# A two-layer hybrid decoder trunk on one core: the order of the memory pools, with TensorE's operands at multiples of 256 bytes

## The chip, the core and the metric

The kernel runs on one core of one Trainium2 chip. The metric is device time in microseconds for one execution, from launch to end; the median of three runs of the kernel before is 1096.18 us (1096.07 to 1096.39). Lower is better.

## The reference: what is computed

The input is one sequence of 512 tokens with 1024 channels in float32. Two layers follow each other. In each layer, `h = RMSNorm(x)`, one combined projection `p = h @ W_in` is cut into the inputs of three mixers and of three merge gates, and the layer ends with a residual:

```
yA = (silu(gate) * B * conv3(C * xA)) @ Wout_A                  # gated convolution of width 3
yB = (sparse attention, 8 heads of 64, times silu(gate)) @ Wout_B
yC = (pooling over windows 2/4/8/16, linear, scale, silu gate) @ Wout_C
x  = x + (sigmoid(gA)*yA + sigmoid(gB)*yB + sigmoid(gC)*yC) @ W_o
```

The attention has rotary positions and normalized queries and keys. A small indexer (8 heads) scores all earlier keys of a query, the 128 best are kept, and the softmax runs over those.

## The kernel before, in words

Everything is held transposed: channels on the 128 partitions, the 512 tokens along the free axis. A float32 product is made of three TensorE matmuls on float32r parts: each operand is split into a high part (a rounded copy) and a low part (the rest), and `mm3` adds high x high, high x low and low x high into one PSUM tile of 128 x 512. `mm` (line 385) issues each of them. In the profile's names, `pj<-xhi,whi` is a matmul into the PSUM tile `pj` whose moving operand is `xhi` (512 columns) and whose stationary operand, loaded by a separate LDWEIGHTS, is 128 columns (512 bytes of a partition) of `whi`.

The weights come as 90 chunks of 128 x 1024 float32 a layer, in their order of use. `prep` loads a chunk into `raw` on the SP queue, ScalarE copies it to `whi` (line 368) and VectorE makes `wlo` (line 369); two raw and three split chunks are held at a time. `project` multiplies one chunk with the eight k tiles of the layer's input: `xhi0..7` and `xlo0..7`, written by `load_x`, each 2048 bytes of a partition. That is 24 matmuls of 512 columns for a chunk, 65 times a layer. The output products of the three branches (`merge`) and of the layer (`project(src)`) take the same weights against tiles `b` (8192 bytes, four slices of 512 columns). The value projection ("v" below) turns this round: there `whi` and `wlo` move, 512 columns at a time, and 128-column slices of `xhi` and `xlo` are loaded as weights. The selection of keys (16 rounds of MAX8 and MATCH_REPLACE8 for each of three query blocks) and the splits run on VectorE beside the matmuls.

The order of instructions on each engine is not the program's: class `Order` plays a list schedule with costs for each instruction and fixes it with edges. It looks at tiles, tags and buffer numbers, and not at where a tile lies in memory.

A tile pool takes a stretch of each partition in the order in which the pools are opened, and in a pool each tag takes its buffers in the order of first use, each rounded up to 32 bytes. The first free byte is 16512. This gives these starts (bytes in a partition, and what is left over a multiple of 256):

| tile | start before | over 256 |
|---|---|---|
| ct (cos, sin, identity, ones, masks), 6212 bytes | 16512 | 128 |
| vt | 22752 | 224 |
| xhi0, xlo0, ss, xhi1, xlo1 ... (17 tiles, 2048 bytes apart) | 22976 | 192 |
| ob (the ones and block matrices) | 57792 | 192 |
| raw, whi, wlo (4096 bytes each) | 63584, 71776, 84064 | 96 |
| b (8 of 8192 bytes), k | 96352, 161888 | 96 |
| a, w, h | 178272, 186464, 200800 | 96 |
| z (3 of 2112 bytes) | 208992 | 96, 160, 224 |
| pth (2 of 6656 bytes) | 215328, 221984 | 32 |

The identity matrix of the transposes (line 388, `pt<-ct,a`) is a part of `ct` and begins at 20608, 128 over a multiple of 256.

Of the kernel before, what the change touches and what calls it, by code (L numbers as in the profile page):

```python
# [5 lines left out]
F32 = mybir.dt.float32  # L6
F32R = mybir.dt.float32r
AF = mybir.ActivationFunctionType
ALU = mybir.AluOpType
PSUM = bass.MemoryType.PSUM  # L10
# [3 lines left out]
P = 128  # L14
S = 512
# [6 lines left out]

# constant columns
C_COS, C_SIN, C_ID, C_ONE, C_BLK, C_CAU, C_INV, C_EPS, C_END = (
    0, 512, 1024, 1152, 1280, 1408, 1536, 1552, 1553)
# per-layer vector columns
V_G, V_CW, V_PS, V_QG, V_KG, V_END = 0, 8, 20, 24, 26, 28


class Order:  # L30
    """The order of the instructions on each engine: a list schedule of the traced program.

    An instruction's place is found from the data it needs, the slots its tiles need and what it
    costs; edges without semaphores then keep each engine to that order."""

    # us from the end of an instruction to the start of one that waits for it
    LAT = {"PE": 0.2, "DVE": 0.13, "Activation": 0.14, "Pool": 0.1, "SP": 0.13}
# [20 lines left out]
    @staticmethod  # L58
    def region(ap):
        """partitions and elements of a tile that an access touches"""  # L60
        t, ap, off = ap.tensor, [list(x) for x in ap.ap], ap.offset
        row = 1
        for n in t.shape[1:]:
            row *= n
        if ap[0][0] != row:
            return t.name, (0, 1 << 30), {0: None}
        p, f = divmod(off, row)
        mask = 1
        for step, n in ap[1:]:
            m = 0  # L70
            for i in range(n):
                m |= mask << (i * step)
            mask = m
        return t.name, (p, p + ap[0][1]), mask << f
# [33 lines left out]
    def cost(self, inst, kind):  # L108
        """us on the engine, and us until the result is there"""
        def size(a):  # L110
            n = 1
            for _, k in a.bass_ap.ap[1:]:
                n *= k
            return n

        aps = [a for a in inst.ins if hasattr(a, "bass_ap")]
        out = inst.outs[0]
        n = size(out)
        psum = any(a.bass_ap.tensor.name.split("_")[0] in ("pj", "sc", "pt", "pv") for a in aps)
        wide = [a for a in aps if size(a) > 1]  # L120
        extra = len(aps) > len(wide)
        engine = str(inst.engine).split(".")[-1]
        if kind == "InstMatmult":
            f32 = str(aps[0].dtype).endswith("float32")
            c = (0.0004167 * n + 0.003) * ((4 if n > 128 else 2) if f32 else 1)
            return c, 0.0
        if kind == "InstDMACopy":
            b = n * out.bass_ap.ap[0][1] * 4
            return (0.65 if aps[0].bass_ap.tensor.name in self.slot else 0.48), b / 360e3
        if engine == "Activation":  # L130
            return 0.093 - 0.042 * psum + 0.000833 * n + 0.093 * extra, 0.0
        if engine == "Pool":
            return (0.1 if kind == "InstMemset" else 0.1 + 0.0022 * n), 0.0
        if kind in ("InstMax", "InstMatchReplace"):
            return 0.069 + 0.00104 * max(size(a) for a in aps), 0.0
        fast = kind == "InstTensorScalarPtr" and len(wide) == 1 and not psum
        return 0.069 + 0.00104 * n * (0.5 if fast else 1) + 0.061 * extra, 0.0
# [109 lines left out]
    def arrange(self, passes=PASSES):  # L247
        raw = self.read()
        ops, users, seqs, place = [], {}, {}, {}
# [23 lines left out]
        for k in range(passes):  # L273
            total, begin, end, order, why = self.play(ops, costs, succ, prio, users)
            if best is None or total < best[0]:
                best = (total, order, begin, end)
            # when each instruction has to start so that the tensor engine never waits
            need = [0.0] * n
# [24 lines left out]
def trunk(ctx, tc, xT, wst, vecs, cst, outT):  # L303
    nc = tc.nc
    order = Order(tc)
    pool = lambda name, bufs, **kw: order.pool(ctx.enter_context(tc.tile_pool(name=name, bufs=bufs, **kw)), name, bufs)
    cp = pool("cp", 1)
    wp = pool("wp", 3)
    bp = pool("bp", 8)
    wk = pool("wk", 7)  # L310
    sm = pool("sm", 4)
    pp = pool("pp", 4, space=PSUM)
    dp = pool("dp", 1, space=bass.MemoryType.DRAM)

    dve, act, pe, gp = nc.vector, nc.scalar, nc.tensor, nc.gpsimd

    ct = cp.tile([P, C_END], F32, name="ct")
    vt = cp.tile([P, DEPTH, V_END], F32, name="vt")
# [7 lines left out]
    def nm(s):  # L326
        uid[0] += 1
        return f"{s}_{uid[0]}"
# [24 lines left out]

    # ---- weight stream: chunks in their order of use, split into two float32r parts
    wq = {}
# [24 lines left out]
    def evac(out, ps, by):  # L380
        """PSUM to SBUF"""
        dve.tensor_tensor(out=out, in0=ps, in1=by, op=ALU.mult)  # L382
# [20 lines left out]
    def mm2(ps, lhs, src):  # L403
        """product with a matrix of ones and zeros"""
        hi, lo = W(F32R), W(F32R)
        split(hi, lo, src)
        mm(ps, lhs, hi, True, False)
        mm(ps, lhs, lo, False, True)
# [3 lines left out]
    def load_x(l, k, xt):  # L412
        """the two parts of x*g for the projections, and the running sum of squares"""
        g = vt[:, l, V_G + k:V_G + k + 1]
        hi = cp.tile([P, S], F32R, name=nm("xhi"), tag=f"xhi{k}")
        lo = cp.tile([P, S], F32R, name=nm("xlo"), tag=f"xlo{k}")
        split(hi, lo, xt, g)
        xh[k] = (hi, lo)
        sq = A()
        act.activation(sq, xt, AF.Square)  # L420
        if k == 0:
            xh["ss"] = cp.tile([P, S], F32, name=nm("ss"), tag="ss")
            gp.tensor_copy(xh["ss"], sq)
        else:
            gp.tensor_tensor(out=xh["ss"], in0=xh["ss"], in1=sq, op=ALU.add)

    def rsqrt(dst, ps, inv_n):
        """the table's value and a Newton step"""
        s, y, h = W(), W(), W()
# [7 lines left out]

# [1 line left out]
    load(vt, vecs)  # L439
# [21 lines left out]
    def wavefront(n, src, head):  # L461
        """n projections at once, whose last source tile comes late"""
        ws = [take() for _ in range(n)]
# [8 lines left out]
    for l in range(DEPTH):  # L472
        # ---- index projections
        ps_ik, pa0, pb0 = wavefront(3, lambda k: xh[k], l == 0)
# [3 lines left out]
        def rope(A, B, c, s, gA=None, gB=None):  # L478
            """-> A*c - B*s, B*c + A*s"""
            t = [W() for _ in range(4)]  # L480
# [17 lines left out]
        def move(pairs):  # L498
            """copies between partitions"""
            for d, u in pairs:  # L500
                load(d.bitcast(F32), u.bitcast(F32))
# [6 lines left out]

        # the indexer's r of the query is left to iw: relu(r s) w = relu(s) (r w)
        iq = [stack(*rope(pa0, pb0, cos, sin))]  # L510
# [8 lines left out]
        pa = project()  # L519
        # ik: x1 in rows 0:32, x2 in rows 32:64; iw in rows 64:72  # L520
        tk = [W() for _ in range(4)]
# [15 lines left out]
        def columns():  # L537
            """r and the heads' weights with tokens on partitions"""
            pw = pt()
# [9 lines left out]

        # ---- index scores and the selection, as an additive bias per query block  # L550
        bias = [cau] + [cp.tile([P, (b + 1) * P], F32, name=nm("score"), tag=f"score{b}") for b in range(1, 4)]
# [25 lines left out]
        def silu2(ps, out=None):  # L577
            """2 * silu(r * ps)"""
            g = W()
# [30 lines left out]

        # ---- pooling branch
        pwh, pwl = take()
# [39 lines left out]

        # ---- queries, keys, values
        def normed(gcol, then):
# [35 lines left out]

        # v, tokens on partitions; a head's 128 columns are [hi lo]
        vps = [pj(), pj(), pj(), pv()]
# [16 lines left out]
        def attention(qd, q, khh, kll):  # L709
            pts, prs = {}, {}  # L710

            def scores(j, b):
# [6 lines left out]
                mn = sm.tile([P, 1], F32, name=nm("mn"), tag="mn")  # L719
                # -(s + bias)/8, and its minimum  # L720
                dve.tensor_tensor_reduce(out=pr[:, :w], in0=ps[:, :w], in1=bias[b], scale=-0.125, scalar=3.0e38,  # L721
# [7 lines left out]
            def turn(j, b):  # L729
# [4 lines left out]
                for c in range(b + 1):  # L734
                    transpose(pst[:, c, :], pr[:, c * P:(c + 1) * P])
                # block (b, c) lies at 3c + b
                dh, dl = (t[:, b:b + 3 * b + 1:3, :] for t in pts[j])
# [28 lines left out]

        # ---- gate of the attention branch (its output replaces it)
        yb = big(F32)
# [5 lines left out]

        # ---- convolution branch
        yh, yl = big(), big()
# [32 lines left out]

        # ---- output projection and residual  # L810
        src = lambda k: (mh[k // 4][:, k % 4, :], ml[k // 4][:, k % 4, :])
# [19 lines left out]
def _columns():  # L831
    """column numbers of w_in, a list of 128 (or fewer) per projection tile, in their order of use"""
    import numpy as np
# [107 lines left out]
```

## Time and profile before

| | |
|---|---|
| median of the runs, us | 1096.18 |
| span of the profiled execution, us | 1093.9 |
| TensorE (PE) busy, us | 1082.8 |
| TensorE weight load (PEld) busy, us | 877.7 |
| VectorE (DVE) busy, us | 800.0 |
| ScalarE (ACT) busy, us | 465.8 |
| GpSimd (POOL) busy, us | 96.9 |
| DMA, mean GB/s | 114 |

The profiled execution's own time is its span, 1093.9 us, and about 2.3 us around it that the records don't cover (the runs agree within 0.3 us of each other). The busy time of PE counts each matmul from its start to its modelled end; matmuls overlap, so a single one shows 390 to 400 ns while the next one starts after 225 to 240 ns. The distance from one start to the next, called the pitch below, is what a matmul costs in a dense stretch.

### The profile page before, as it was taken

What the parts mean: (1) busy time and instruction counts of PE and PEld (TensorE: products, weight loads), DVE (VectorE), ACT (ScalarE), POOL (GpSimd) and SP (SyncE); (2) the same over time, 40 slices, a digit from 0 to 9 for tenths busy, and PEclk for the clock granted to TensorE, in tenths of its full rate; (3) what the DMA queues carried; (4) which work ended last, traced back from release to release, by engine and by line L of the source; (5) the groups of instructions that cost most, each with busy time, mean ns of one, the idle gap of its engine ahead of it and who ended that gap; (6) DMA issues with size and microseconds to landing.
All of it is one profiled execution on the core that took longest, in us unless ns stands there. A gap on an engine that the chain in (4) does not pass through costs nothing.

```text
span 1093.9 us, 13444 instructions
## 1 busy us (share of the span) xinstructions
PE 1082.8 (99%) x4842; PEld 877.7 (80%) x4842; DVE 800.0 (73%) x1389; ACT 465.8 (43%) x747; POOL 96.9 (9%) x76
## 2 busy tenths in 40 slices
PE   7999999999999999999999999999999999999998
PEld 5788888888888888888887778888888878888887
DVE  6989999987558865455559899999776498744442
ACT  6355222485223673233334542235852347623320
POOL 4000000000000011221310000000000001121310
PEclk9999999999999999999999999999999999999999
DMA  6542222452224522234535322225423245132252
GB/s 222 162 128 78 96 97 95 132 147 70 82 98 130 160 72 80 94 97 161 166 116 150 116 84 94 96 78 163 126 77 97 78 138 151 59 96 96 96 192 77
DMA packets 44402, 124.39 MB, mean 114 GB/s; under 512 B 6960, under 2 KB 7472, under 8 KB 44336
## 3 DMA queue, kind: packets, MB, share of 16 engines
q1 hardware_dynamic: 44336, 123.53, 35.9%
q8 instruction: 38, 0.62, 0.2%
q14 instruction: 28, 0.23, 0.1%
HBM read 101.49 MB, written 4.19 MB: 97 GB/s over the span
## 4 chain that ended last, share of the span: by engine, by line
PE 97%; DVE 1%; DMA 1%; ACT 1%; SPq 0%; issue 0%; DVEq 0%
PE pj L385 88%; PE sc L385 4%; PE pv L385 3%; PE pt L388 2%; DMA b<-in_x 0%; DVE wlo L369 0%; SPq L352 0%; DMA k<-h 0%; ACT xhi L400 0%; ACT whi L368 0%; DVE h L398 0%; DVE xlo L401 0%; ACT a L420 0%; DVE w L646 0%; DVE w L816 0%
## 5 line engine op out<-in xcount | busy, mean ns | idle before, releaser
L385 PE MATMUL pj<-xhi,whi 128*128 128x512 f32 x1040 | 378.1, 398 | 6.2 <-ACT whi L368 6.2
L385 PE MATMUL pj<-xhi,wlo 128*128 128x512 f32 x1040 | 377.5, 397 | 0.2 <-DVE wlo L369 0.2
L385 PE MATMUL pj<-xlo,whi 128*128 128x512 f32 x1040 | 377.3, 397 | 0.0
L368 ACT ACTIVATE whi<-raw 128x1024 fp32r<-128x1024 f32 (+2 forms) x185 | 191.6, 1037 | 403.0 <-PE pj L385 362.9
L369 DVE TENSOR_TENSOR wlo<-raw,whi 128x1024 fp32r<-128x1024 f32 (+2 forms) x185 | 227.7, 1233 | 18.2 <-ACT whi L368 17.2
L385 PEld LDWEIGHTS pj<-xhi,whi 128*128 128x128 f32 x1040 | 194.8, 188 | 50.6 <-ACT whi L368 6.2
L385 PEld LDWEIGHTS pj<-xlo,whi 128*128 128x128 f32 x1040 | 195.2, 188 | 45.5 <-DVE xlo L401 0.5
L385 PEld LDWEIGHTS pj<-xhi,wlo 128*128 128x128 f32 x1040 | 195.3, 188 | 45.3 <-DVE wlo L369 1.4
L385 PE MATMUL pj<-b,whi 128*128 128x512 f32 x640 | 211.2, 391 | 0.0
L382 DVE TENSOR_TENSOR w<-pj,ss 128x512 f32<-128x512 f32 x104 | 71.0, 686 | 99.8 <-PE pj L385 99.0
L385 PEld LDWEIGHTS pj<-b,whi 128*128 128x128 f32 x640 | 119.9, 188 | 25.4
L385 PE MATMUL pj<-b,wlo 128*128 128x512 f32 x320 | 118.5, 392 | 0.0
L607 POOL TENSOR_TENSOR b<-b,w 128x512 f32<-128x512 f32 x32 | 60.7, 1904 | 269.4 <-DVE w L605 269.2
L385 PEld LDWEIGHTS pj<-b,wlo 128*128 128x128 f32 x320 | 60.0, 188 | 12.7
L573 DVE MAX8 m<-score 128x8 f32<-128x256 f32 (+2 forms) x96 | 53.2, 558 | 1.7
L574 DVE MATCH_REPLACE8 score<-m,score 128x384 f32<-128x384 f32 (+2 forms) x96 | 52.1, 543 | 0.0
L739 DVE TENSOR_TENSOR pth<-pt,pth 128x128 fp32r<-128x128 f32 (+1 forms) x64 | 31.1, 486 | 19.0 <-PE pv L385 9.5
L816 DVE TENSOR_TENSOR w<-pj,w 128x512 f32<-128x512 f32 x16 | 11.0, 690 | 45.6 <-PE pj L385 45.6
L724 ACT ACTIVATE a<-a,mn 128x128 f32<-128x128 f32 (+1 forms) x64 | 35.7, 558 | 16.0 <-DVE mn L721 15.5
L662 POOL TENSOR_TENSOR w<-w,w 128x512 f32<-128x512 f32 x8 | 11.3, 1414 | 333.1 <-ACT w L661 333.1
L738 ACT ACTIVATE pth<-pt 128x128 fp32r<-128x128 f32 (+1 forms) x64 | 27.7, 433 | 28.2 <-PE pt L388 20.6
L385 PE MATMUL pv<-pth,b 128*128 128x512 f32 (+3 forms) x128 | 39.7, 314 | 0.0
(119 smaller groups left out, 1002.0 us busy)
## 6 DMA issues: line engine op xcount, KB each, us to landing
raw<-in_w SPq DMA_DIRECT2D x177, 512.0 KB, 3.3
b<-h SPq DMA_DIRECT2D x128, 64.0 KB, 2.3
k<-h SPq DMA_DIRECT2D x64, 128.0 KB, 3.0
b<-in_x SPq DMA_DIRECT2D x8, 256.0 KB, 4.8
w<-in_x SPq DMA_DIRECT2D x8, 256.0 KB, 5.6
xs<-w SPq DMA_DIRECT2D x8, 256.0 KB, 2.4
w<-xs SPq DMA_DIRECT2D x8, 256.0 KB, 4.1
out_x<-w SPq DMA_DIRECT2D x8, 256.0 KB, 2.0
```

The source lines that it names most:

```text
L368: act.activation(hi[:, p], raw[:, p], AF.Copy)
L369: dve.tensor_tensor(out=lo[:, p], in0=raw[:, p], in1=hi[:, p].bitcast(F32), op=ALU.subtract)
L382: dve.tensor_tensor(out=out, in0=ps, in1=by, op=ALU.mult)
L385: pe.matmul(ps, lhs, rhs, start=start, stop=stop)
L388: pe.transpose(out, src, ident if n == P else ident[64:64 + n, 64:64 + n])
L573: dve.max(m8, score)
L574: dve.match_replace(score, m8, score, -3.0e38)
L607: gp.tensor_tensor(out=a, in0=a, in1=g, op=ALU.add)
L662: gp.tensor_tensor(out=s0, in0=s0, in1=s1, op=ALU.add)
L724: act.activation(pr[:, :w], pr[:, :w], AF.Exp, bias=mn, scale=-1.0, accum_out=zs)
L738: act.activation(dh, pst[:, :b + 1, :], AF.Copy)
L739: dve.tensor_tensor(out=dl, in0=pst[:, :b + 1, :], in1=dh.bitcast(F32), op=ALU.subtract)
```

## The change

The pools are opened in another order. A new pool `xp` comes first; it holds one tile `gap` of 128 bytes that nothing writes or reads, and then the tiles `xhi`, `xlo` and `ss`, which were in `cp`. `wp`, `bp` and `wk` follow, and `cp` with the constants stands behind them. The rest of the diff takes comments out of the source.

```diff
@@ trunk
-    cp = pool("cp", 1)
+    xp = pool("xp", 1)
     wp = pool("wp", 3)
     bp = pool("bp", 8)
     wk = pool("wk", 7)
+    cp = pool("cp", 1)
     sm = pool("sm", 4)
...
+    xp.tile([P, 32], F32, name="gap")
     ct = cp.tile([P, C_END], F32, name="ct")
...
@@ load_x
-        hi = cp.tile([P, S], F32R, name=nm("xhi"), tag=f"xhi{k}")
-        lo = cp.tile([P, S], F32R, name=nm("xlo"), tag=f"xlo{k}")
+        hi = xp.tile([P, S], F32R, name=nm("xhi"), tag=f"xhi{k}")
+        lo = xp.tile([P, S], F32R, name=nm("xlo"), tag=f"xlo{k}")
...
-            xh["ss"] = cp.tile([P, S], F32, name=nm("ss"), tag="ss")
+            xh["ss"] = xp.tile([P, S], F32, name=nm("ss"), tag="ss")
```

By the same counting of sizes, the tiles then start here:

| tile | start after | over 256 |
|---|---|---|
| xhi0, xlo0, ss, xhi1 ... (2048 bytes apart) | 16640 | 0 |
| raw, whi, wlo | 51456, 59648, 71936 | 0 |
| b, k | 84224, 149760 | 0 |
| a, w, h | 166144, 174336, 188672 | 0 |
| z | 196864 | 0, 64, 128 |
| pth | 203200, 209856 | 192 |
| ct, vt, ob | 216512, 222752, 222976 | 192, 32, 0 |

No instruction is added, removed or reshaped, and `Order` sees the same tiles, tags and buffer numbers.

## Rows read from the trace of the kernel before

**Rows 1.** The page, parts 1 and 2: PE, and TensorE's granted clock in tenths.
```profile
PE 1082.8 (99%) x4842; PEld 877.7 (80%) x4842; DVE 800.0 (73%) x1389; ACT 465.8 (43%) x747; POOL 96.9 (9%) x76
PEclk9999999999999999999999999999999999999999
```

**Rows 2.** The page, part 4: the chain that ended last, by engine and line.
```profile
PE 97%; DVE 1%; DMA 1%; ACT 1%; SPq 0%; issue 0%; DVEq 0%
PE pj L385 88%; PE sc L385 4%; PE pv L385 3%; PE pt L388 2%; DMA b<-in_x 0%; DVE wlo L369 0%; SPq L352 0%; DMA k<-h 0%; ACT xhi L400 0%; ACT whi L368 0%; DVE h L398 0%; DVE xlo L401 0%; ACT a L420 0%; DVE w L646 0%; DVE w L816 0%
```

**Rows 3.** Waits of PE: waited for, us in total, times, longest.
```profile
PE pj L385 <- ACT whi L368: 6.2, 1, 6.2
```

**Rows 4.** Groups by form, PE and PEld: output<-moving,stationary, shapes, count | busy us, mean ns.
```profile
L385 PE MATMUL pj<-xhi,whi 128*128 128x512 f32 x1040 | 378.1, 398 | 6.2 <-ACT whi L368 6.2
L385 PE MATMUL pj<-b,whi 128*128 128x512 f32 x640 | 211.2, 391 | 0.0
L385 PE MATMUL pj<-b,wlo 128*128 128x512 f32 x320 | 118.5, 392 | 0.0
L385 PE MATMUL pj<-whi,xhi 128*128 128x512 f32 x48 | 17.7, 395 | 0.0
L385 PE MATMUL pv<-whi,xhi 128*128 128x512 f32 x16 | 6.3, 396 | 0.0
L388 PE MATMUL pt<-ct,a 128*128 128x128 f32 x160 | 28.0, 272 | 0.2
L385 PEld LDWEIGHTS pj<-xhi,whi 128*128 128x128 f32 x1040 | 194.8, 188 | 50.6 <-ACT whi L368 6.2
```

**Rows 5.** Timeline of PE, projections alone (start us, us); 15 starts from first to last.
```profile
324.64 0.40 PE L385 MATMUL pj<-xhi,whi 128*128 128x512 f32 x1
...
328.14 0.40 PE L385 MATMUL pj<-xhi,whi 128*128 128x512 f32 x1
```

**Rows 6.** Timeline of PE, output projection alone; 12 starts from first to last.
```profile
544.17 0.39 PE L385 MATMUL pj<-b,wlo 128*128 128x512 f32 x1
...
546.89 0.39 PE L385 MATMUL pj<-b,wlo 128*128 128x512 f32 x1
```

**Rows 7.** Timeline of PE, value projection alone; 14 starts from first to last.
```profile
187.65 0.40 PE L385 MATMUL pv<-whi,xlo 128*128 128x512 f32 x1
...
190.93 0.40 PE L385 MATMUL pv<-whi,xhi 128*128 128x512 f32 x1
```

**Rows 8.** Timeline of PE, both kinds by turns, one matmul each; 14 starts.
```profile
182.57 0.39 PE L385 MATMUL pj<-whi,xhi 128*128 128x512 f32 x1
182.79 0.40 PE L385 MATMUL pj<-xlo,whi 128*128 128x512 f32 x1
...
185.79 0.39 PE L385 MATMUL pj<-wlo,xhi 128*128 128x512 f32 x1
```

**Rows 9.** Timeline of PE: four transposes in a row.
```profile
410.94 0.60 PE L388 MATMUL pt<-ct,a 128*128 128x128 f32 x4
```

**Rows 10.** Windows of 25 us: window, length, busy of PE, PEld, DVE, ACT, POOL.
```profile
0.00:25.00 25.00, 18.56 (x70) 13.91 (x71) 17.59 (x18) 16.61 (x29) 11.63 (x14) 1.00 0.68 231
75.00:100.00 25.00, 25.00 (x116) 20.50 (x116) 24.01 (x43) 16.06 (x31) 0.30 (x3) 1.00 0.19 64
125.00:150.00 25.00, 25.00 (x109) 20.24 (x109) 23.86 (x56) 6.36 (x8) 0.00 (x0) 1.00 0.27 87
150.00:175.00 25.00, 25.00 (x109) 20.19 (x109) 24.11 (x50) 6.36 (x7) 0.00 (x0) 1.00 0.30 103
175.00:200.00 25.00, 25.00 (x109) 20.18 (x108) 24.24 (x41) 10.49 (x15) 2.60 (x2) 1.00 0.28 85
200.00:225.00 25.00, 25.00 (x111) 20.26 (x111) 24.22 (x45) 12.86 (x20) 0.00 (x0) 1.00 0.63 174
675.00:700.00 25.00, 25.00 (x110) 20.21 (x109) 24.19 (x52) 7.84 (x9) 0.00 (x0) 1.00 0.26 91
725.00:750.00 25.00, 25.00 (x108) 20.10 (x108) 24.81 (x41) 10.97 (x15) 1.54 (x1) 1.00 0.41 123
875.00:900.00 25.00, 25.00 (x107) 19.82 (x106) 24.21 (x34) 8.66 (x12) 1.55 (x1) 1.00 0.43 126
```

## The prediction, made blind

> **What bounds the kernel now.** First the page's shares: TensorE has work in 99% of the span, and its granted clock is full, the level of 2.4 GHz, in all 40 slices [rows 1]. Then the chain of waits: 97% of the span lies on PE, 88% on the matmuls into `pj` alone [rows 2]. Then what PE waited for: 6.2 us at the start, once, and next to nothing afterwards [rows 3]. So the matmul stream sets the time, and the question is how long one matmul takes. Its busy time doesn't tell that (398, 391, 395 ns by form [rows 4], longer than the distance between two starts). The distance from start to start, the pitch, is read from the timeline in stretches with one kind of matmul:
>
> - `xhi` or `xlo` moving, weights from `whi` or `wlo`: 3.50 us over 15 starts, 233.3 ns [rows 5].
> - `b` moving, weights again from `whi` or `wlo`: 2.72 us over 12 starts, 226.7 ns [rows 6].
> - `whi` or `wlo` moving, weights from slices of `xhi` or `xlo`: 3.28 us over 14 starts, 234.3 ns [rows 7].
>
> All three stream 512 columns, which at 2.4 GHz are 213.3 ns; so each matmul pays 13 to 21 ns more than its columns. The kinds differ in nothing that the array sees. What differs is where the operands start: `x` tiles 192 bytes over a multiple of 256; `whi`, `wlo` and `b` 96 over. When both operands are at 96, the extra is 13.4 ns; with the moving one at 192 it is 20.0; with the stationary one at 192 it is 21.0.
>
> One more stretch narrows it. At 182.57 us the two kinds alternate: while an `x` tile streams, the weights loaded for the next matmul come from `x`, and while `whi` streams, the next weights come from `whi`. There the two streams that are read at the same time always have the same offset, and the pitch is 3.22 us over 14 starts, 230.0 ns [rows 8]: exactly between 226.7 and 233.3. If only the difference of the two offsets counted, this stretch would run at 226.7. So the offset itself counts, the worse of the two operands sets the price, and 192 is worse than 96.
>
> **The change, part by part.** No instruction is added, removed or moved on any queue, and the planner doesn't see addresses, so the order on every engine and the list of loads stay. What changes is the start of the tiles: `x` from 192 to 0 over a multiple of 256; `raw`, `whi`, `wlo`, `b`, `k`, `a`, `w`, `h` from 96 to 0; `pth` from 32 to 192; the constants from 128 to 192. All operands of the three stretches above come to 0, which no moving tile of 512 columns has now. What is the pitch there? The trace bounds it:
>
> - Below by the columns: 213.3 ns. The nearest row to this end is the transposes: their moving operand, the identity, starts at 128 over a multiple of 256, the nearest to 0 that exists. Four take 0.60 us [rows 9] and one lasts 0.272 [rows 4], so the pitch is (0.60 - 0.272)/3 = 109 ns, 2.3 ns over two clock cycles for each of the 128 columns. That is another mode, so I don't take its 2.3 ns as the price.
> - Above, for a gain, by the best kind now: 226.7 ns. Above that, for a loss, by the worst kind now, 234.3 ns.
>
> Which value? Counted from the nearest multiple of 128, 192 is 64 away and costs 20.0 to 21.0 ns; 96 is 32 away and costs 13.4. One step of 32 bytes is worth 6.6 ns. One step more, to 0 away, gives 13.4 - 6.6 = 6.8 ns, a pitch of 220.1; I take 220 ns. It lies in the middle between the two bounds for a gain (213.3 and 226.7), and both stay in the range.
>
> The terms at 220 ns:
>
> - Projections: three forms of 1040 [rows 4] are 3120 matmuls. The first 70 fall in the first 25 us, where PE waits for loads and splits (18.56 us busy of 25 [rows 10]), and gain nothing. 3050 x (233.3 - 220) ns = 40.6 us.
> - Value projection: three forms of 48 and three of 16 [rows 4], 192 x (234.3 - 220) = 2.7 us.
> - Products from `b`: 640 + 320 [rows 4], 960 x (226.7 - 220) = 6.4 us. Where `b` and `x` matmuls take turns the two pitches mix, and their sum stays the same.
> - By the loops there are 140 more of 512 columns (scores, values, sums of squares, pool mixing) and narrower ones; those with `pth` keep a bad offset. At 6.7 ns the 140 would bring 0.9 us; I leave it out.
>
> Sum: 49.7 us. Then what is late next. VectorE makes `wlo` and shares its time with the key selection; its work doesn't shrink. A window of 25 us of projections would take 25 x 220/233.3 = 23.57 us, and eight windows hold more VectorE work than that: 24.01, 23.86, 24.11, 24.24, 24.22, 24.19, 24.81 and 24.21 [rows 10]. The excess is 0.44 + 0.29 + 0.54 + 0.67 + 0.65 + 0.62 + 1.24 + 0.64 = 5.1 us; there PE will wait for VectorE, and I take it off in full. The weight load is no such cover: 188 ns [rows 4] lies within a pitch of 220.
>
> ScalarE, VectorE, GpSimd and the loads get other addresses too. I cost that at nothing: PE hides them (waits of 6.2 us in all [rows 3]). Were VectorE 1% slower or faster by its addresses, the eight windows would move by 8 x 0.24 = 2 us either way; that stays in the range.
>
> Net 49.7 - 5.1 = 44.6 us. The profiled execution is its span of 1093.9 us and 2.3 us around it, 1096.2, which is the median of the runs; 1096.2 - 44.6 = **1052 us**, 4.1% faster.
>
> The page SBUF — State Buffer of the Trainium skill speaks against any of this: in its section Who interferes with whom, PE has two independent read ports for the moving operand and the weights, and never waits on anyone; the section Operand start alignment asks only for a multiple of the element size, and says that nothing was timed there. By this page alone the sum would be zero; the 226.7 against 234.3 ns of two stretches that both move tiles at offset 96 shows a dependence that it doesn't have.
>
> **The rivals.**
>
> 1. *No extra at all is left.* With aligned operands the stream runs at its columns plus the transposes' 2.3 ns, 215.6 ns. For it: the transposes. Against it: they are another mode, and no 512-column stretch comes near. 3050 x 17.7 + 192 x 18.7 + 960 x 11.1 ns = 54.0 + 3.6 + 10.7 = 68.3 us. A window then wants 23.10 us, and VectorE holds 0.91 + 0.76 + 1.01 + 1.14 + 1.12 + 1.09 + 1.71 + 1.11 = 8.9 us back in the eight: 59.4 us net, **1037 us**. The Trainium skill's page TensorE: Matmul & The Clock Gate, section Back-to-back issue gap, gives N/2.4 + 2.5 ns, some 216 for 512 columns, and names no address; before the change no stretch here follows it.
>
> 2. *226.7 ns is the floor.* The 13.4 ns that are left when both operands are at 96 belong to changing weights and not to the offset; the aligned tiles only reach the better of the present classes. For it: two very steady levels, 226.7 and 233.3 to 234.3, and nothing lower in a dense stretch. 3050 x 6.6 + 192 x 7.6 ns = 20.1 + 1.5 = 21.6 us; one window (24.81 against 25 x 226.7/233.3 = 24.29) takes 0.5 back: **1075 us**.
>
> 3. *Slower: multiples of 64 are the bad class.* The `x` tiles, slow now, start at a multiple of 64 (192), the fast ones 32 beside one (96). If that is the rule, as of two streams meeting in the same part of the memory, the change moves `whi`, `wlo` and `b` into the bad class and leaves `x` in it: 960 x (233.3 - 226.7) = 6.3 us more, **1102.5 us**. For it: the order of the two levels as they stand, and that in rows 8 the `x` half, both streams on multiples of 64, must run at 233.3. Against it: the identity at 128, a multiple of 64 too, with its 2.3 ns. The point from which it decides: the gains and losses cancel where the pitch at 0 is the present mean, (3120 x 233.3 + 192 x 234.3 + 960 x 226.7)/4272 = 231.9 ns.
>
> 4. *It is not the address* but, say, how the tiles are written, and the levels stay: **1096 us**.
>
> **How the numbers follow.** Forecast 0.40; rival 1 0.22; rival 2 0.22; rival 3 0.11; rival 4 0.05. A gain in three cases of 0.84 together. A measurement of this kernel can tell about 0.2% (2 us) from no change; so faster 0.84, same 0.05, slower 0.11. The likeliest case's own range goes from half way to rival 1 to half way to rival 2, 1044 to 1063. The range that holds 8 in 10 takes in both rivals and the 2 us for VectorE's addresses, and for rival 1 that VectorE's excess is made up in neighbouring windows (8.9 us, to 1028): 1030 to 1080. It leaves out no change and slower (0.16).
>
> **What would show it.** In the profile after, the timeline of the same three stretches should show one pitch for all kinds, near 220 ns, with the counts of all forms unchanged. 215 to 217 is rival 1, 226 to 227 rival 2, 233 and `b` slower rival 3. PE's waits for `wlo` from VectorE, absent now, should appear in the stretches of the key selection and come to about 5 us; if they are far larger, VectorE has become the bound and my sum is too good. The prediction is wrong if the pitch of the kinds still differs, or if the stretches agree and the total doesn't follow.

## The result: 1078.9 us, and the profile after

The changed kernel takes 1078.91 us (median; 1078.84 to 1079.16) against 1096.29 us of the kernel before on the same chip: ratio 0.9839, 95% interval 0.9825 to 0.9853, a gain of 17.4 us. The forecast was 1052 us. So the direction was right and the size was not: the gain is less than half of the 44.6 us forecast, and nearest to rival 2 (1075 us). The time lies just inside the range that was to hold 8 in 10 (1030 to 1080), at its far end, and outside the 1044 to 1063 of the likeliest case.

The page of the kernel after, parts 1, 2 and 4, as in [rows 1] and [rows 2]:

```profile
span 1077.1 us, 13444 instructions
PE 1065.4 (99%) x4842; PEld 878.4 (82%) x4842; DVE 799.2 (74%) x1389; ACT 465.5 (43%) x747; POOL 97.2 (9%) x76
PEclk9999999999999999999999999999999999999999
PE 96%; DVE 1%; DMA 1%; issue 0%; ACT 0%; SPq 0%; DVEq 0%; ACTq 0%
```

The same instructions, the same clock, the same bound; only PE's busy time is 17.4 us less. The lines of the source have moved by three, so L388 is what L385 was. The timeline of PE after, in the same three kinds of stretch and the alternating one as [rows 5 to 8]: projections (15 starts from first to last), output projection (12), value projection (14), both by turns (14).

```profile
315.21 0.39 PE L388 MATMUL pj<-xhi,whi 128*128 128x512 f32 x1
...
318.61 0.39 PE L388 MATMUL pj<-xhi,whi 128*128 128x512 f32 x1
...
536.21 0.39 PE L388 MATMUL pj<-b,wlo 128*128 128x512 f32 x1
...
538.93 0.39 PE L388 MATMUL pj<-b,wlo 128*128 128x512 f32 x1
```

```profile
178.88 0.39 PE L388 MATMUL pj<-wlo,xhi 128*128 128x512 f32 x1
...
182.05 0.39 PE L388 MATMUL pv<-whi,xlo 128*128 128x512 f32 x1
...
183.64 0.39 PE L388 MATMUL pj<-whi,xhi 128*128 128x512 f32 x1
...
186.81 0.39 PE L388 MATMUL pv<-wlo,xhi 128*128 128x512 f32 x1
```

3.40 us over 15, 2.72 over 12, 3.17 over 14 (by turns) and 3.17 over 14 (values): 226.7, 226.7, 226.4 and 226.4 ns, one pitch for all kinds within what two digits can tell. (The two stretches of 14 mix matmuls into `pj` and `pv`; the operands are those named.) The projections came down from 233.3, the values from 234.3 and the alternating stretch from 230.0; the products from `b` stayed exactly where they were. That is the picture that the prediction named for rival 2.

What PE waited for, against [rows 3]:

```profile
PE pj L388 <- ACT whi L371: 6.5, 1, 6.5
PE sc L388 <- DVE w L649: 0.6, 1, 0.6
PE sc L388 <- DVE w L401: 0.3, 1, 0.3
PE sc L388 <- DMA k<-h: 0.2, 1, 0.2
```

No wait for `wlo` appeared. The 5.1 us that VectorE was to hold back belonged to a pitch of 220 ns that PE never reached.

### The profile page after: what moved, and what is told of

Read it like the earlier page. It is cut to its first block, busy times and chain, and to the rows that moved or that the text cites. A ratio compares the mean times of both kernels' runs of the same rounds, so it can differ in the third digit from the quotient of the medians.

```text
span 1077.1 us, 13444 instructions
## 1 busy us (share of the span) xinstructions
PE 1065.4 (99%) x4842; PEld 878.4 (82%) x4842; DVE 799.2 (74%) x1389; ACT 465.5 (43%) x747; POOL 97.2 (9%) x76
## 4 chain that ended last, share of the span: by engine, by line
PE 96%; DVE 1%; DMA 1%; issue 0%; ACT 0%; SPq 0%; DVEq 0%; ACTq 0%
PE pj L388 87%; PE sc L388 4%; PE pv L388 3%; PE pt L391 2%; DMA b<-in_x 0%; DVE wlo L372 0%; DMA k<-h 0%; DVE w L488 0%; SPq L355 0%; DVE h L401 0%; ACT whi L371 0%; DVE w L649 0%; ACT xhi L403 0%; DVE w L435 0%; DVE w L436 0%
## 5 line engine op out<-in xcount | busy, mean ns | idle before, releaser
L388 PE MATMUL pj<-xhi,whi 128*128 128x512 f32 x1040 | 373.1, 393 | 6.5 <-ACT whi L371 6.5
L388 PE MATMUL pj<-xlo,whi 128*128 128x512 f32 x1040 | 372.8, 393 | 0.0
L388 PE MATMUL pj<-xhi,wlo 128*128 128x512 f32 x1040 | 372.4, 393 | 0.0
L388 PEld LDWEIGHTS pj<-xhi,whi 128*128 128x128 f32 x1040 | 195.0, 188 | 46.7 <-ACT whi L371 6.7
L388 PEld LDWEIGHTS pj<-xhi,wlo 128*128 128x128 f32 x1040 | 195.7, 188 | 39.4 <-DVE wlo L372 0.5
L388 PEld LDWEIGHTS pj<-xlo,whi 128*128 128x128 f32 x1040 | 195.5, 188 | 39.4
L388 PE MATMUL pj<-b,whi 128*128 128x512 f32 x640 | 210.7, 390 | 0.0
L385 DVE TENSOR_TENSOR w<-pj,ss 128x512 f32<-128x512 f32 x104 | 70.8, 684 | 93.3 <-PE pj L388 93.0
L388 PEld LDWEIGHTS pj<-b,whi 128*128 128x128 f32 x640 | 120.0, 188 | 24.2
L388 PE MATMUL pj<-b,wlo 128*128 128x512 f32 x320 | 118.2, 391 | 0.0
L388 PEld LDWEIGHTS pj<-b,wlo 128*128 128x128 f32 x320 | 60.1, 188 | 12.3
L665 POOL TENSOR_TENSOR w<-w,w 128x512 f32<-128x512 f32 x8 | 11.9, 1492 | 325.4 <-ACT w L664 325.4
L388 PE MATMUL pv<-pth,b 128*128 128x512 f32 (+3 forms) x128 | 39.9, 316 | 0.0
L741 ACT ACTIVATE pth<-pt 128x128 fp32r<-128x128 f32 (+1 forms) x64 | 27.6, 432 | 27.4 <-PE pt L391 20.1
```

What stands on the lines that cost most here:

```text
L388: pe.matmul(ps, lhs, rhs, start=start, stop=stop)
L665: gp.tensor_tensor(out=s0, in0=s0, in1=s1, op=ALU.add)
L741: act.activation(dh, pst[:, :b + 1, :], AF.Copy)
```

## The experiments

Theory A is the prediction's: the offset of an operand over a multiple of 256 bytes counts by itself, and the worse of the two sets the price. Its rival, theory B: only the difference between the offsets of the moving and the stationary operand counts. Both allow the result in kind: the change made all offsets 0, and with that equal. (The prediction's 220 ns at 0/0 was out with the result; in what follows theory A has the measured 226.7 ns there.)

### Bare matmuls at chosen offsets

A kernel with nothing but stretches of 48 matmuls, 512 columns and 128 columns of weights unless said otherwise, each stretch on its own source line; `mo` and `so` are the bytes of the moving and the stationary operand over a multiple of 256. An offset pair is written moving/stationary below, so 192/0 is the stretch of L58. The weights alternate between two slices 512 bytes apart.

```
    run(lambda *a: nc.tensor.matmul(*a[:3], start=a[3], stop=a[4]), mo=192, so=0)     # L58
    run(lambda *a: nc.tensor.matmul(*a[:3], start=a[3], stop=a[4]), mo=192, so=192)   # L72
```

> A kernel of bare matmul stretches (48 matmuls of 512 columns each on float32r, weights of 128 columns, both operands at chosen byte offsets over a multiple of 256; it computes nothing of the reference and copies the input to the output). Theory A, the offset itself counts and the worse operand sets the price: pitch 226.7 ns at 0/0 (moving/stationary) and 96/96, 233 at 192/192, 233 at 192/0, 234 at 0/192; by turns 192/96 and 96/192: 230; by turns 192/192 and 96/96: 233 to 234. Theory B, only the difference of the two offsets counts: 226.7 on the whole diagonal (32/32 to 224/224), 233 to 234 wherever the two differ. Theory C, the 13.4 ns that are left at 0/0 are the price of changing the weights: about 13 ns over the columns also at 384 and 256 columns, and less with 64 or 32 columns of weights. Against C, the 13.4 ns belong to the moving columns: 10 ns at 384, 6.7 at 256, and the same with 64 columns of weights.

The timeline of PE, one row for a stretch (start us, us). From one row's start to the next's, divided by 48, is the pitch, the first few starts of a new stretch included. L58 is 192/0, L61 0/64 and L65 0/192; L72 is 192/192; L76 and L77 alternate, 192/96 with 96/192 and 192/192 with 96/96; L80 is 256/0; L83 and L84 have both at 0 with 384 and 256 columns, L87 both at 192 with 448; L91 is bf16, both at 0 (one record of its 48 is missing).

```profile
86.77 11.35 PE L58 MATMUL ps<-mv,st 128*128 128x512 f32 x48
97.97 11.35 PE L59 MATMUL ps<-mv,st 128*128 128x512 f32 x48
...
120.34 11.36 PE L61 MATMUL ps<-mv,st 128*128 128x512 f32 x48
131.54 11.40 PE L62 MATMUL ps<-mv,st 128*128 128x512 f32 x48
...
165.14 11.16 PE L65 MATMUL ps<-mv,st 128*128 128x512 f32 x48
176.13 11.37 PE L66 MATMUL ps<-mv,st 128*128 128x512 f32 x48
...
241.91 11.08 PE L72 MATMUL ps<-mv,st 128*128 128x512 f32 x48
252.82 11.07 PE L73 MATMUL ps<-mv,st 128*128 128x512 f32 x48
...
286.16 11.21 PE L76 MATMUL ps<-mv,st 128*128 128x512 f32 x48
297.22 11.40 PE L77 MATMUL ps<-mv,st 128*128 128x512 f32 x48
308.45 11.51 PE L78 MATMUL ps<-mv,st 128*128 128x512 f32 x48
...
330.92 11.09 PE L80 MATMUL ps<-mv,st 128*128 128x512 f32 x48
341.85 11.04 PE L81 MATMUL ps<-mv,st 128*128 128x512 f32 x48
...
363.94 8.48 PE L83 MATMUL ps<-mv,st 128*128 128x384 f32 x48
372.27 5.91 PE L84 MATMUL ps<-mv,st 128*128 128x256 f32 x48
378.01 8.51 PE L85 MATMUL ps<-mv,st 128*128 128x384 f32 x48
...
392.11 9.89 PE L87 MATMUL ps<-mv,st 128*128 128x448 f32 x48
401.84 11.20 PE L88 MATMUL ps<-mv,st 128*64 128x512 f32 x48
...
435.05 10.53 PE L91 MATMUL ps<-mh,sh 128*128 128x512 bf16 x47
445.42 10.52 PE L92 MATMUL ps<-mh,sh 128*128 128x512 bf16 x47
```

At 192/192 the pitch is 10.91 us over 48, 227.3 ns, and at 32, 64, 96, 128, 160 and 224 it is within 0.2 ns of that (once settled, the starts lie 226 and 227 ns apart, at 0/0 too). At 160/0, 192/0 and 224/0 it is 234.2, 233.3 and 232.9; at 0/64 233.3. One difference lies between: the moving operand 64 ahead, 229.0 ns at 0/192, and 229.2 at 64/0. A moving operand at 256 or 512 against weights at 0 runs at 227.7 and 226.9, as equal; so the difference counts over 256 bytes. For stretches that keep one pair of offsets theory B holds and theory A falls: 192 isn't a bad place, nor 0 a good one.

The two alternating stretches came out as theory A had them, and not as B: 230.4 ns for 192/96 by turns with 96/192, where B has 233 to 234, and 234.0 for 192/192 by turns with 96/96, where every matmul has equal offsets and B has 226.7. So the offsets of a matmul's neighbours count too; the part on why the prediction was wrong comes back to this.

Theory C holds in its first half at 384 and 256 columns: with equal offsets the extra over the columns is 13.5 ns (8.33 us over 48 less 160.0) and 12.9 (5.74 over 48 less 106.7). At 448 columns, both operands at 192, it is 16.0 (9.73 over 48 less 186.7), which neither side of C expected. Its second half doesn't hold: with 64 and 32 columns of weights the pitch is no lower, 229.8 and 231.7 ns.

In bf16 the pitch is 216.0 ns (10.37 us over 48) at 0/0, and its settled starts lie 216 ns apart at 192/192 too; unequal offsets were not run in bf16. The trace agrees with the formula N/2.4 + 2.5 ns, some 216 for 512 columns, that the Trainium skill states in TensorE: Matmul & The Clock Gate, section Back-to-back issue gap, for a single matmul; for a stream of weight loads and matmuls, as here, that section states some 131 ns, and no stretch of 512 columns here comes near it. At 512 columns float32r doesn't reach 216 ns at any offset tried.

### Everything at 192

```diff
-    xp.tile([P, 32], F32, name="gap")
+    xp.tile([P, 16], F32, name="gap")
```

> The kernel after with a gap of 64 bytes instead of 128: all of TensorE's operands lie 192 over a multiple of 256 (a multiple of 64) instead of 0. Theory A (offset itself, 192 is a bad one): every kind at 233 to 234 ns, 1100 to 1103 us. Theory B (only the difference of the offsets): 226.7 ns as after, 1079 us.

1079.34 us, ratio to before 0.9847 (0.9831 to 0.9863): the same as after within the noise. The timeline of PE, projections; 15 starts in 3.40 us, 226.7 ns:

```profile
315.69 0.39 PE L388 MATMUL pj<-xhi,whi 128*128 128x512 f32 x1
...
319.09 0.39 PE L388 MATMUL pj<-xhi,whi 128*128 128x512 f32 x1
```

The `x` tiles lie at 192 again, where they cost 233.3 ns in the kernel before, and run at the good pitch, because the weights lie there too.

### The new order without the gap

```diff
-    xp.tile([P, 32], F32, name="gap")
```

> The kernel after without the gap: the new order of the pools alone, all of TensorE's operands at 128 over a multiple of 256. Theory A with distances from a multiple of 128: as after, 226.7 ns, 1079 us. Theory A with distances from a multiple of 256: the worst place, 234 ns or more, 1100 us or more. Theory B: 226.7 ns, 1079 us.

1079.04 us, ratio 0.9846 (0.9831 to 0.9860). Multiples of 256 have no part in the gain; 128 does as well.

### The old order, aligned

```diff
     vt = cp.tile([P, DEPTH, V_END], F32, name="vt")
+    cp.tile([P, 16], F32, name="gap")
...
+    wp.tile([P, 24], F32, name="gap2", tag="gap2", bufs=1)
     uid = [0]
```

> The kernel before with its order of pools (constants first) and two gaps, 64 bytes before the x tiles and 96 before raw, so that x, whi, wlo and b all start at a multiple of 256. If the alignment is all of the gain: 226.7 ns in every stretch and 1079 us, as after. If the order of the pools has a part in it (the distance of the tiles from each other, or the constants behind): between 1079 and 1096 us.

1078.88 us, ratio 0.9845 (0.9830 to 0.9859). The order of the pools has no part in it either.

### The x tiles 64 bytes ahead of the weights, or behind

The gap between the `x` tiles and the weights, 192 bytes for the first kernel and 64 (16 columns) for the second:

```diff
-    xp.tile([P, 32], F32, name="gap")
...
+    wp.tile([P, 48], F32, name="gap", tag="gap", bufs=1)
     uid = [0]
```

> The kernel after with its gap moved: none ahead of the x tiles, 192 bytes between them and the weights, so x starts 64 bytes further than whi, wlo and b over a multiple of 256 (128 against 64); all starts are still multiples of 64. Theory B with the period of 256 bytes, by the bare stretches: projections 228.9 ns (moving 64 ahead), values 233.4 (moving 64 behind), b 226.7: 1079 + 3050 x 2.2 ns + 192 x 6.7 ns = 1087 us, or 1085 if again a fifth of it is lost. Rival, a period of 64 bytes: 1079 us as after.

> The same with 64 bytes between x and the weights: x at 128, whi, wlo and b at 192, x 64 bytes behind. Theory B with the period of 256 bytes: projections 233.4 ns, values 228.9, b 226.7: 1079 + 3050 x 6.7 ns + 192 x 2.2 ns = 1100 us, or 1096 if a fifth is lost: all of the gain gone although every operand starts at a multiple of 64. Rival, a period of 64 bytes: 1079 us.

Ahead: 1089.25 us, ratio 0.9941 (0.9924 to 0.9957). Behind: 1094.24 us, ratio 0.9984 (0.9975 to 0.9994). All starts are multiples of 64 in both, so a period of 64 bytes is out. The timeline of PE, projections (15 starts) and values (12), ahead and then behind:

```profile
316.29 0.39 PE L388 MATMUL pj<-xhi,whi 128*128 128x512 f32 x1
...
319.72 0.39 PE L388 MATMUL pj<-xhi,whi 128*128 128x512 f32 x1
...
188.97 0.39 PE L388 MATMUL pv<-whi,xhi 128*128 128x512 f32 x1
...
191.77 0.63 PE L388 MATMUL pj<-whi,xhi 128*128 128x512 f32 x2
```

```profile
315.82 0.40 PE L388 MATMUL pj<-xhi,whi 128*128 128x512 f32 x1
...
319.32 0.39 PE L388 MATMUL pj<-xhi,whi 128*128 128x512 f32 x1
...
189.18 0.39 PE L388 MATMUL pv<-whi,xhi 128*128 128x512 f32 x1
...
191.93 0.62 PE L388 MATMUL pj<-whi,xhi 128*128 128x512 f32 x2
```

Ahead: 228.7 and 233.3 ns. Behind: 233.3 and 229.2. These are the pitches that the bare stretches gave, with the sides changed as they should, though not everywhere: over the whole trace the projections ahead average 229.4 ns in their pure stretches, and the values behind 231.2. The totals were missed: ahead is 2 to 4 us worse than expected and behind 2 to 6 better. The sums take each matmul by its own operands and leave out what the stretches cost where `x` and `b` take turns. Ahead, matmul for matmul against the kernel after, the 632 distances between an `x` and a `b` matmul grew from 227.0 to 231.6 ns on average, 2.9 us, where the sum has 0.7: that covers the 2 us by which it was missed. Behind, the kernel before is the better measure, for its projections and `b` have the same pitches: of the 1.7 us between the medians (1.5 between the traces), the turns of `x` and `b` make 1.1 and the values 0.5; the other pieces are smaller and of both signs.

### Is there a better difference than none?

> A second kernel of bare matmul stretches (it computes nothing of the reference). Theory B: with the weights at 0, every moving offset from 8 to 240 bytes that is no multiple of 64 costs 230 to 237 ns, none goes below 226.7; equality over 256 bytes is the best place there is. Rival: some small difference (8 to 56 bytes) lets the two reads miss each other and falls below 226.7, towards the 215.8 of bf16. By columns: at a difference of 192 or 128 the extra over the columns is either fixed (20 ns at 512, 384 and 256 columns, so a price for each weight load) or grows with the columns (15 ns at 384, 10 at 256). Loading the same weights every time: 226.7 as before if the load is done each time anyway. Weights with a step of two elements: read over twice as many bytes, so they leave the common offset, 230 or more; or 226.7 if only the start counts.

Seventeen more differences between 8 and 240 bytes ran: none is below equality. The lowest is 12 bytes with 229.0 ns, the highest 120 bytes with 240.0, both outside the 230 to 237 expected. (The first kernel had two more: 236.7 at 4 bytes, 231.5 at 16.) The timeline of these two (L55, L65), of stretches at a difference of 192 with 384 and 256 columns (L71, L72), of two more alternating stretches (L75: 192/96 with 96/96, L76: 0/0 with 0/192) and of the same weights each time (L77):

```profile
43.74 11.15 PE L55 MATMUL ps<-mv,st 128*128 128x512 f32 x48
54.73 11.37 PE L56 MATMUL ps<-mv,st 128*128 128x512 f32 x48
...
155.10 11.68 PE L65 MATMUL ps<-mv,st 128*128 128x512 f32 x48
166.62 11.36 PE L66 MATMUL ps<-mv,st 128*128 128x512 f32 x48
...
222.67 8.64 PE L71 MATMUL ps<-mv,st 128*128 128x384 f32 x48
231.15 5.82 PE L72 MATMUL ps<-mv,st 128*128 128x256 f32 x48
236.80 8.59 PE L73 MATMUL ps<-mv,st 128*128 128x384 f32 x48
...
250.92 11.22 PE L75 MATMUL ps<-mv,st 128*128 128x512 f32 x48
261.98 11.20 PE L76 MATMUL ps<-mv,st 128*128 128x512 f32 x48
273.02 11.05 PE L77 MATMUL ps<-mv,st 128*128 128x512 f32 x48
283.90 11.36 PE L78 MATMUL ps<-mv,st 128*128 128x512 f32 x48
```

At a difference of 192 the extra grows with the columns: 16.7 ns at 384 (8.48 us over 48, less 160.0) and 11.0 at 256 (5.65 over 48, less 106.7), against 20.0 at 512. At a difference of 128 it is 15.6 and 11.9. With 256 columns a difference is even cheaper than equality, 117.7 against 119.6 ns. Loading the same weights again costs the same, 226.7 ns. Weights with a step of two elements, from the same start as the moving operand, take 233.3 ns: the common start alone is not enough.

Of the alternating stretches, L75 lies half way between its two kinds (230.4 ns), but L76 is dearer than either of its kinds alone: 230.0 ns, where 0/0 takes 226.7 and 0/192 229.0.

### One gap in the kernel before

Where theories A and B differ most, in the whole kernel and with one line: the `x` tiles stay, and the weights and `b` come to their offset, the one that theory A calls bad.

```diff
+    wp.tile([P, 24], F32, name="gap", tag="gap", bufs=1)
     uid = [0]
```

> The kernel before with one line more: 96 bytes of gap between the constants' pool and raw. The x tiles stay where they were, 192 over a multiple of 256; raw, whi, wlo and b move from 96 to 192, the offset of x. Theory B (the difference of the two offsets counts): 226.7 ns in every stretch and 1079 us, as after. Theory A as the prediction had it (the offset itself counts, 192 is worse than 96): the projections stay at 233.3, b rises to 233.3, 1102 us.

1078.94 us, ratio 0.9846 (0.9832 to 0.9859): the whole gain of the change, with 96 bytes of gap. Its projections, 15 starts in 3.40 us, 226.7 ns:

```profile
316.08 0.39 PE L386 MATMUL pj<-xhi,wlo 128*128 128x512 f32 x1
...
319.48 0.39 PE L386 MATMUL pj<-xhi,wlo 128*128 128x512 f32 x1
```

## Why the prediction was wrong

**What held.** The bound (the matmul stream), the three pitches, the finding that addresses set them, and the direction. The direction was luck in part: the change made the offsets equal in making them 0, and any other common offset would have brought the same. Rival 3 was wrong: two stretches of bare float32r matmuls that differ in one address run at 227.3 (192/192) and 233.3 ns (192/0), and the slower has the stationary operand at 0, the faster has both at 192. The page SBUF — State Buffer of the Trainium skill (section Who interferes with whom), by which PE has two independent read ports and never waits, has no such dependence; the measurement decides.

**The step that failed** is "So the offset itself counts, the worse of the two operands sets the price", and from it "One step of 32 bytes is worth 6.6 ns. One step more, to 0 away, gives 13.4 - 6.6 = 6.8 ns". A line was drawn through two points that don't lie on a common scale. 96/96 was cheap for being equal, 192/96 and 96/192 dear for being unequal; at 0/0 there was no further step to take. In place of 220 ns the runs showed 226.7 at 0/0, and the same at 192/192, the offset that the prediction called the worse: in the bare stretches, in the whole kernel at 192, and in the kernel before with the weights moved to 192. The rows for the right reading were there: the best of the three kinds was the only one with equal offsets.

It was the alternating stretch [rows 8] that turned the argument away from the difference. It was read as "equal at any time, and yet 230.0". The bare stretches repeat it: 192/96 by turns with 96/192, so that a stream and the weights loaded for the next matmul are equal, takes 230.4 ns (11.06 us over 48), and 192/192 by turns with 96/96 takes 234.0. Being equal with the next weights alone gives half of the gain, being equal with the own weights alone none; all of it came only where every matmul of a stretch had the one offset. Nor is the 230.0 one pitch: in the kernel before, the distance after an `x` tile streams is 234.5 ns on average and after a `whi` or `wlo` tile 226.1 (19 of each), and in the bare stretch 236 and 224. That is what theory A would have, and so the trace before alone could not decide between the two. Which reads of three successive matmuls meet was not settled.

**The terms.** Projections: 40.6 us forecast at 13.3 ns each. Matmul for matmul, in the order that both traces share, the 3000 whose distance to the next start is below 260 ns in both went from 233.2 to 227.6 ns on average, 16.9 us. The pure stretches fell by 6.6, as rival 2 has it; next to transposes and shorter matmuls less. Values: 2.7 us forecast, 1.1 measured. Products from `b`: 6.4 forecast; the 945 with dense distances gave 1.2 us, most of it in the stretches that they share with `x`. All dense distances together gave 19.1 us. VectorE's 5.1 us didn't come.

**What was given back.** The other 165 distances grew by 2.0 us in sum. At the start the kernel after falls behind by 1.2 us: its matmuls lie 427 ns apart, 512 columns at the lower level of 1.2 GHz, until about 12 us, those of the kernel before only until about 9 (the granted clock in the profile's rows reads 1.00 there all the same, so the level is read from the 427 ns). But the kernel before has longer distances of its own between 17 and 23 us, and by the 70th matmul, at 25 us, nothing of this is left. What is left comes later, in single places: a matmul before a sum of squares that waits for its operand, 0.71 us where it was 0.40, another before a score, 0.64 where it was 0.44, and a number of smaller ones, each under 0.15 us.

With the stream's first matmul 0.3 us later, 19.1 less 2.0 makes the 16.8 us by which the two profiled spans differ. The medians differ by 17.4, because the profiled execution before, with 1093.9, was among the quicker ones: other executions of that kernel have spans of 1093.6 to 1094.7 us, about 1.8 below their times, so the 2.3 us that the prediction adds to the span is some 0.5 too much. Rival 2's 21.1 us fell short by these 2.0 and by what its projections lost next to other matmuls (16.9 against 20.1 us); the 1.2 from `b` made up a part.

**The chances.** The size that came had a chance of 0.22 in the prediction, as rival 2, and the forecast of 0.40 rested on the extrapolation alone. Rival 2 had the size, but not the cause: it took the new offset for one of a better class, where only its being common counted, and it gave the remaining 13.4 ns to changing weights, while loading the same weights again costs just as much.

## What to carry to other kernels

Where float32r matmuls of 512 columns follow each other densely, look at the pitch by kind of operands, and let all the moving and stationary tiles of the stretch start at one common offset over 256 bytes; here that took 6.7 ns off a projection's matmul, and one gap of 96 bytes did it. Two levels that go with two addresses say nothing yet about a third address: put both operands on the same bad offset first, which costs one line and tells the offset from the difference.

## What the runs showed of the hardware

- For float32r in stretches that keep one pair of offsets, the difference of the two operands' starts, taken over 256 bytes, sets the pitch at 512 columns: 226.7 ns when equal (eight offsets), about 229 with the moving operand 64 bytes ahead or 12 ahead, 230 to 240 at the others tried, most of them 233 to 234.
- Where pairs of offsets take turns, the neighbours count: 192/192 by turns with 96/96 takes 234.0 ns though each matmul's own offsets are equal, and 0/0 by turns with 0/192 takes 230.0, more than either alone. The rule behind this stays open.
- When equal, the price over the columns is 13 to 14 ns for a matmul at 512, 384, 320 and 256 columns, but 16.0 at 448; at a difference of 192 it grows with the columns (11.0, 16.7 and 20.0 ns at 256, 384 and 512), and at 256 columns this difference is cheaper than equality (117.7 against 119.6 ns).
- In bf16 the price was 2.7 ns: 216 ns at 0/0 and at 192/192. What the 13 ns of float32r are for stays open; fewer columns of weights didn't lower them (229.8 ns with 64), nor did loading the same weights again (226.7).
